# Fetches in tasks of their own, an output norm in place and convolution taps from the bank, in a two-layer encoder trunk

## The chip, the cores and the metric

One core of one Trainium2 chip runs the whole program as one launch. The metric is device time in microseconds, median of the runs. The engines named below are TensorE (matmuls and transposes, PE in the rows; PEld is its weight load), VectorE (DVE), ScalarE (ACT), GpSimd (POOL) and SyncE (SP), which issues every DMA of this kernel. Each engine works through its own list of instructions in order.

## The reference, cut to what matters

Two layers over 2048 frames of width 1024, float32. Each layer normalises its input, projects it once, runs two groups of four heads on the projection, and adds an output projection to its input.

```python
def hybrid_layer(x, ...):
    proj = rmsnorm(x, norm_w) @ w_in          # split: mq mk mv mi mf mz | aq ak av az
    qk = silu(causal_conv(concat(mq, mk), conv_w, conv_b))     # 4 taps, depthwise
    hm = mlstm_chunkwise(mq_c, mk_c, mv, mi + i_bias, mf + f_bias)
    ym = (rmsnorm(hm, m_norm_w) + m_skip * mq_c) * silu(mz)
    ha = diff_attention(rope(aq), rope(ak), av, lam)           # softmax1 - lam*softmax2, causal by chunks of 64
    ya = rmsnorm(ha, a_norm_w) * (1 - lambda_init) * silu(az)
    return x + concat(ym, ya) @ w_out
```

A final norm closes the trunk.

## The kernel before

Rows are worked in stages of 512 frames: 2 layers x 4 stages. A stage has 4 units, one per head u of both groups, so there are 32 units. A unit has projections (convolution of q and of k, the two gates, the values and the rotated q and k of the next unit), scores and softmax maps of the attention head, its product with V, and the mLSTM recurrence over four blocks of 128. After unit 3 of a stage the first half of the output projection (`outproj`, units 0 and 1) runs, merged with `prep_t`, which brings the next stage's 512 x 1024 rows in, scales them by their row norm (line 258), transposes them on TensorE and splits them into a high part (line 264) and a low part (line 266). The second half of the output projection runs in unit 1 of the next stage.

Every float32 matmul is made of three matmuls of split operands. Weights come by DMA into `wr` and are split by ScalarE (line 184) and GpSimd (line 186).

The PSUM banks with the tag `mm` are three; all projections, the output projection and the transposes of `prep_t` take turns in them. Tags in `BUFS` say how many buffers a tile name has: `x` (rows of the next stage) 4, `bc` (row factors of the recurrence) 1, `gza` (the attention gate) 1, `yta` (the normed attention output) 1, `tmp` 4, `yha` and `yla` (the split output of a unit) 2.

Around the change:
- `prep_t`, lines 255 to 259: at the first and the fifth of its eight tasks four half-rows of 128 x 512 are issued and multiplied, and the transposes of four tasks read them.
- `proj_conv`, lines 382 to 396: ScalarE copies the finished bank into `raw` behind three halo columns, which frees the bank; VectorE makes a first pass (line 390) and three taps (line 393) from `raw`; `silu2` follows, whose first step is line 374 on ScalarE.
- `mlstm.begin`, lines 535 to 551: the row factors, 512 KB, are read back from DRAM with a broadcast (line 537), and VectorE (line 539) and ScalarE (line 543) use them at once. For unit 0 they are written in the gates of the same stage (line 515).
- `finish`, lines 762 to 793: `factors` multiplies the attention output with the gate into `yta` (line 778); `spread`, planned 5.5 later, multiplies it with the row norms and splits it (lines 612 and 614). The next unit's gate is written at line 375.

The order comes from a plan. The loop at the end of `trunk_kernel` puts each task at a planned time, tasks are emitted in the order of these times, and matmuls of one stream keep that order. Inside these bounds a scheduler orders each engine's instructions by priority and by readiness in its own model of durations.

Of the kernel before, what the change touches and what calls it, by code (L numbers as in the profile page):

```python
# [38 lines left out]
VD = 3.0  # L39
VL = 0.6  # L40
FD = 5.5
MD = 9.0
MS = 4.2
HA = 150

# [5 lines left out]
def trunk_kernel(ctx, tc, x, w_ch, w_v0, w_v, w_o, nw, cw, cb, gb, mnw, msk, anw, lam,  # L51
# [7 lines left out]
    dr = ctx.enter_context(tc.tile_pool(name="dr", bufs=1, space=bass.MemoryType.DRAM))  # L59

    BUFS = dict(x=4, hth=8, htl=8, wr=3, wh=3, wl=3, yhm=3, ylm=3, yha=2, yla=2, kc=1, vc=2,
                kp=3, vp=3, q=2, raw=1, p=15, ath=2, atl=2, ab=2, tmp=4, xr=2, bc=1, ot=1, ytm=1, yta=1,
                mq=1, mk=1, gzm=1, gza=1, vaug=2, st=1, kw=1, hs=1, hsn=1, aj=1)
    PB = dict(mm=3, sc=2, tpa=1, pv=1, ml=1)

# [40 lines left out]
    def tr(o, i, n=P):  # L106
        pin(PE.transpose(o, i, ident[:n, :n]))  # L107
# [132 lines left out]
    def prep_t(l, t, rs, H, rows=None):  # L240
        pr = par[l]
        src = xin(l, t)
        xs = []

        def task(dc):
            def f():
                if dc == 0:
                    H["rope"] = sb.tile([P, 2, T], F32, tag="rope", name="rope", bufs=1)
                    SY.dma_start(H["rope"], rope[t])
                half, j = divmod(dc, 4)  # L250
                if rows:
                    xs[:] = [r_[half] for r_ in rows]
                elif j == 0:
                    xs.clear()
                    for tb in range(4):
                        xt = st([P, T], "x")
                        SY.dma_start(xt, src[tb * P:(tb + 1) * P, half * T:(half + 1) * T])
                        V.tensor_scalar(out=xt, in0=xt, scalar1=rs()[tb], scalar2=None, op0=ALU.mult)
                        xs.append(xt)
                ps = pst("mm", [P, T])  # L260
                for tb in range(4):
                    tr(ps[:, tb * P:(tb + 1) * P], xs[tb][:, j * P:(j + 1) * P])
                h = st([P, T], "hth", F32R)
                A.activation(h, ps, AF.Copy, scale=pr["nw"][:, dc:dc + 1])
                lo = st([P, T], "htl", F32R)
                V.scalar_tensor_tensor(out=lo, in0=ps, scalar=pr["nw"][:, dc:dc + 1], in1=f32(h),
                                       op0=ALU.mult, op1=ALU.subtract)
                H["hh"].append(h)
                H["hl"].append(lo)
            return f  # L270

        return [(0.44, task(dc)) for dc in range(8)]


# [102 lines left out]
    def proj_conv(l, u, qk, H, X):  # L377

        pr = par[l]

        def post(ps):
            halo = pr["halo"][u]
            raw = st([P, T + 3], "raw")
            A.activation(raw[:, 3:], ps, AF.Copy)
            A.activation(raw[:, 0:3], halo[:, qk], AF.Copy)
            A.activation(halo[:, qk], raw[:, T:], AF.Copy)
            ch = qk * NH + u
            w = lambda j: pr["cw"][:, ch * 4 + j:ch * 4 + j + 1]
            acc = st([P, T], "tmp", name="cacc")
            V.tensor_scalar(out=acc, in0=raw[:, 3:], scalar1=w(3), scalar2=pr["cb"][:, ch:ch + 1],  # L390
                            op0=ALU.mult, op1=ALU.add)
            for j in (2, 1, 0):
                V.scalar_tensor_tensor(out=acc, in0=raw[:, j:j + T], scalar=w(j), in1=acc, op0=ALU.mult, op1=ALU.add)  # L393
            nm = "mq" if qk == 0 else "mk"
            X[nm] = st([P, T], nm)
            silu2(X[nm], acc)

        return proj_ch(l, u, qk, H, post)
# [132 lines left out]
    def mlstm(l, u, X, Y):  # L531
        pr = par[l]
        c = {}

        def begin():
            bc = st([P, 2, 4, P], "bc")
            SY.dma_start(bc.rearrange("p a b i -> p a (b i)"), Y["bwd"][:, u * T:(u + 1) * T].partition_broadcast(P))
            c["dec"] = sm(4, "dec")
            V.tensor_copy(c["dec"], bc[:, 1, :, P - 1])
            wt = c["wt"] = bc[:, 0]  # L540
            cols = Y["cols"]
            for tb in range(4):
                A.activation(wt[:, tb], wt[:, tb], AF.Exp, bias=cols[:, 4 * u + tb:4 * u + tb + 1])
            G.affine_select(out=wt, in_=wt, pattern=[[0, 4], [1, P]], compare_op=ALU.is_ge, fill=0.0,
                            base=0, channel_multiplier=-1)
            c["qw"] = bc[:, 1].rearrange("p b i -> p (b i)")
            G.tensor_tensor(c["qw"], c["qw"], X["mq"], op=ALU.mult)
            c["sk"] = st([P, T], "ytm")
            A.activation(c["sk"], X["mq"], AF.Copy, scale=pr["msk"][:, u:u + 1])
            c["hs"] = st([P, 4, P + 1], "hs")  # L550
            c["ss"] = sm(4, "mss")
# [53 lines left out]
        ts_ = []  # L605
        for tb in range(4):
            ts_ += [lambda tb=tb: s1(tb), lambda tb=tb: s2(tb)]
        return begin, ts_, norm, out_

    def split_y(y, kind):  # L610
        yh = st([P, T], "yh" + kind, F32R)
# [145 lines left out]
    def finish(l, t, u, X):  # L757

        pr = par[l]
        c = {}  # L760

        def factors():

            ot, zz = X["ot"], X["zz"]
            ss = sm(4, "ass")
            ps = pst("tpa", [P, 4, P])
            for qb in range(4):
                tr(ps[:, qb], ot[:, qb * P:(qb + 1) * P])
            for qb in range(4):
                junk = st([P, P], "aj", BF16)  # L770
                A.activation(junk, ps[:, qb], AF.Square, accum_out=ss[:, qb:qb + 1])  # L771
            r = c["r"] = sm(4, "ar")
            V.tensor_tensor(r, zz[:, :, 0], zz[:, :, 0], op=ALU.mult)
            V.tensor_scalar(out=ss, in0=ss, scalar1=1.0 / P, scalar2=None, op0=ALU.mult)
            V.scalar_tensor_tensor(out=r, in0=r, scalar=EPS, in1=ss, op0=ALU.mult, op1=ALU.add)
            G.tensor_tensor(r, r, mhalf, op=ALU.pow)
            y = c["y"] = st([P, T], "yta")
            V.scalar_tensor_tensor(out=y, in0=ot, scalar=pr["anw"][:, 0:1], in1=X["gza"], op0=ALU.mult, op1=ALU.mult)
            if (l, t, u) == units[-1]:

                X["r"] = r
                X["ya"] = split_y(y, "a")

        def spread():

            if (l, t, u) == units[-1]:
                return
            y = c["y"]
            ps = pst("tpa", [P, 4, P])
            for qb in range(4):  # L790
                tr(ps[:, qb], c["r"][:, qb:qb + 1].to_broadcast([P, P]))
            V.tensor_tensor(y, y, ps.rearrange("p a b -> p (a b)"), op=ALU.mult)
            X["ya"] = split_y(y, "a")

        return factors, spread


# [161 lines left out]
    for k in range(-1, N + 1):  # L959
# [6 lines left out]
        if k >= 1:  # L966
# [7 lines left out]
            at(fin_t[k - 1], spread, "V")  # L974
            att += 1.1 * len(v1) + 0.88
        segs = []
        tm = None
        if cur:
            l, t, u = cur
            s = l * n_t + t  # L980
            H, X = Hs[s], Xs[k]
            q0, q1 = scores(l, t, u, X, 0), scores(l, t, u, X, 1)
            v0 = apply_v(l, t, u, X, 0)
            att += total(q0) + total(q1) + 1.1 * len(v0)
            if u == 2 and s < last:
                at(xc, lambda s=s: rs0.__setitem__(s + 1, prep_x((s + 1) // n_t, (s + 1) % n_t)))
            segs.append((0.0, proj_conv(l, u, 0, H, X) + proj_conv(l, u, 1, H, X)))
            if u == 1 and s > 0:
                pl, pt_ = divmod(s - 1, n_t)
                segs.append((fin_t[k - 2] + 6.0, outproj(pl, pt_, 1, Xs[k - 3:k - 1])))  # L990
                if pl == n_layers - 1:
                    segs.append((0.0, [(0.0, lambda pl=pl, pt_=pt_: final(pl, pt_))]))
            segs.append((0.0, proj_gate(l, u, 2, H, X, "gzm")))
            segs.append((0.0, proj_gate(l, u, 3, H, X, "gza")))
            if u == NH - 1 and s < last:
                op = outproj(l, t, 0, Xs[k - 3:k - 1])
                segs.append((fin_t[k - 2] + 6.0, op[:len(op) // 4]))

                pt = prep_t((s + 1) // n_t, (s + 1) % n_t, lambda s=s: rs0[s + 1], Hs[s + 1])
                segs.append((0.0, merge(pt, op[len(op) // 4:])))  # L1000
        elif k == -1:
            segs.append((0.0, prep_first(Hs[0])))
        if nxt:
# [17 lines left out]
        rate = (pe + att) / pe if pe else 1.0  # L1021
        for i, (nb, g) in enumerate(segs):
            xc = max(xc, nb)
            xc = put(g, xc, xc + total(g) * rate)
            if i == 0:
                tm = xc
# [3 lines left out]
        if cur:  # L1030
# [10 lines left out]
            if u == 0:  # L1041
                a = max(t0 + 0.5, me_)
                for g in gates(l, t, X, Ys[s]):
                    at(a, g)
                    a += 3.5
                a = max(a, tm + MD)
            begin, ms, norm, out_ = mlstm(l, u, X, Ys[s])
            at(a, begin)
            a += 4.5
            for f in ms:  # L1050
# [99 lines left out]
```

## Time and profile before

| what | value |
|---|---|
| median of 3 runs | 2933.03 us (2927.04 to 2936.75) |
| the profiled execution's own time | 2937.63 us |
| its span, first to last instruction | 2935.9 us |
| TensorE busy | 2711.7 us, 92% |
| VectorE busy | 1952.4 us, 66% |
| ScalarE busy | 1643.6 us, 56% |
| GpSimd busy | 1467.7 us, 50% |
| mean granted TensorE clock | 0.968 of full speed |

Times in the rows are microseconds from the start of the span, durations of one instruction in a group are nanoseconds. An engine that is idle before an instruction waits for another engine or a DMA, which the rows name behind an arrow.

### The profile page before, as it was taken

The page shows a single profiled execution, that of the slowest core. Times are in us where ns is not written, and L with a number is a line of the kernel's source. Part 1 is how long each engine was busy: PE and PEld are TensorE (multiplying, and loading weights), DVE is VectorE, ACT ScalarE, POOL GpSimd, SP SyncE. Part 2 cuts the span into 40 slices and gives each one's busy share as a digit, 9 for nine tenths or more (in the row PEclk, how much of TensorE's full clock was granted, in tenths as well). Part 3 has the DMA queues.
Part 4 walks back from the last instruction along what each step waited for, and adds up shares of the span by engine and source line. Part 5 has one row for each costly group of instructions (what it writes and reads, how often), then busy time and mean ns, then how long its engine had stood idle before and what let it go on. Part 6 is the DMA issues. An engine that isn't in the chain of part 4 may idle for free. (4 is left out here: it accounts for less than half of the span.)

```text
span 2935.9 us, 48969 instructions
## 1 busy us (share of the span) xinstructions
PE 2711.7 (92%) x16692; PEld 2395.2 (82%) x16692; DVE 1952.4 (66%) x4695; ACT 1643.6 (56%) x4471; POOL 1467.7 (50%) x1182
## 2 busy tenths in 40 slices
PE   7999899999999899999999999999989998998997
PEld 5788788887887888888888887888878887887877
DVE  5566576676757767567855566766677677776684
ACT  4555465555655556555555454555455555665564
POOL 5565656544454344434455655555543545435324
PEclk9999999999999999999999999999999999999998
DMA  6545654463544444434446454654546444364232
GB/s 197 156 130 162 183 157 149 142 200 109 173 140 126 155 116 140 117 99 133 145 130 184 135 175 137 196 167 144 166 127 218 137 140 140 110 186 143 83 107 87
DMA packets 241755, 428.91 MB, mean 146 GB/s; under 512 B 30304, under 2 KB 92768, under 8 KB 241504
## 3 DMA queue, kind: packets, MB, share of 16 engines
q1 hardware_dynamic: 241504, 425.77, 48.5%
q8 instruction: 132, 2.16, 0.3%
q14 instruction: 119, 0.97, 0.1%
HBM read 312.28 MB, written 63.05 MB: 128 GB/s over the span
## 5 line engine op out<-in xcount | busy, mean ns | idle before, releaser
L186 POOL TENSOR_TENSOR wl<-wr,wh 128x512 fp32r<-128x512 f32 (+1 forms) x676 | 919.1, 1366 | 1113.2 <-ACT wh L184 508.5
L104 PE MATMUL mm<-hth,wh 128*128 128x512 f32 x1536 | 629.8, 410 | 1.9 <-ACT vaug L327 1.4
L184 ACT ACTIVATE wh<-wr 128x512 fp32r<-128x512 f32 (+1 forms) x676 | 421.2, 627 | 354.8 <-PE mm L104 219.4
L104 PE MATMUL mm<-htl,wh 128*128 128x512 f32 x1536 | 617.6, 402 | 0.0
L692 DVE TENSOR_SCALAR_CACHE_REDUCE p<-sc 128x512 f32<-128x512 f32 (+3 forms) x640 | 382.0, 605 | 135.0 <-PE sc L104 113.3
L655 ACT ACTIVATE p<-p,nm 128x512 f32<-128x512 f32 (+3 forms) x640 | 413.5, 649 | 102.2 <-DVE nm L651 101.8
L104 PE MATMUL mm<-hth,wl 128*128 128x512 f32 x1536 | 449.8, 407 | 0.0
L104 PEld LDWEIGHTS mm<-hth,wh 128*128 128x128 f32 x1536 | 296.3, 193 | 61.6 <-ACT vaug L327 1.6
L104 PEld LDWEIGHTS mm<-hth,wl 128*128 128x128 f32 x1536 | 291.7, 195 | 62.5 <-POOL wl L186 0.2
L104 PEld LDWEIGHTS mm<-htl,wh 128*128 128x128 f32 x1536 | 295.9, 193 | 57.1
L669 DVE SCALAR_TENSOR_TENSOR p<-p,s 128x512 f32<-128x512 f32 (+2 forms) x320 | 303.0, 992 | 2.1
L104 PE MATMUL mm<-wh,hth 128*128 128x256 f32 (+1 forms) x1024 | 269.0, 292 | 18.4 <-DVE gt L329 10.9
L741 ACT ACTIVATE ath<-tpa 128x512 fp32r<-128x512 f32 x288 | 170.1, 590 | 185.3 <-PE tpa L107 184.4
L742 DVE TENSOR_TENSOR atl<-tpa,ath 128x512 fp32r<-128x512 f32 x288 | 196.9, 684 | 111.9 <-ACT ath L741 110.4
L104 PE MATMUL mm<-wh,htl 128*128 128x256 f32 (+1 forms) x1024 | 264.8, 288 | 0.0
L104 PE MATMUL sc<-kp,q 128*128 128x512 f32 x768 | 247.3, 409 | 7.0 <-DVE p L692 6.8
L393 DVE SCALAR_TENSOR_TENSOR cacc<-raw,cw,cacc 128x512 f32<-128x512 f32 x192 | 218.8, 1140 | 4.4
L104 PEld LDWEIGHTS mm<-wh,hth 128*128 128x128 f32 x1024 | 199.4, 195 | 24.5 <-issue 9.4
L104 PEld LDWEIGHTS mm<-wh,htl 128*128 128x128 f32 x1024 | 199.5, 195 | 2.6
L107 PE MATMUL tpa<-ident,p 128*128 128x128 f32 x1088 | 189.7, 281 | 9.2 <-DVE tpa L734 7.6
L104 PE MATMUL pv<-ath,vp 128*128 128x256 f32 x768 | 181.7, 290 | 7.3 <-ACT ath L741 7.2
L104 PE MATMUL mm<-wl,hth 128*128 128x256 f32 (+1 forms) x1024 | 164.2, 289 | 0.0
(203 smaller groups left out, 5684.2 us busy)
## 6 DMA issues: line engine op xcount, KB each, us to landing
wr<-in_w_ch_dram SPq DMA_DIRECT2D x384, 256.0 KB, 2.8
wr<-in_w_o_dram SPq DMA_DIRECT2D x132, 256.0 KB, 2.9
q<-ab SPq DMA_DIRECT2D x256, 128.0 KB, 2.4
vp<-vd SPq DMA_DIRECT2D x48, 512.0 KB, 4.0
wr<-in_w_v_dram SPq DMA_DIRECT2D x96, 256.0 KB, 3.0
kp<-kd SPq DMA_DIRECT2D x48, 512.0 KB, 4.2
wr<-in_w_v_dram SPq DMA_DIRECT2D x64, 264.0 KB, 3.4
kc<-ab SPq DMA_DIRECT2D x256, 64.0 KB, 2.0
```

The source lines that it names most:

```text
L104: pin(PE.matmul(o, l, r, start=start, stop=stop, skip_group_check=True))
L107: pin(PE.transpose(o, i, ident[:n, :n]))
L184: A.activation(wh[:, :n], wr[:, :n], AF.Copy)
L186: G.tensor_tensor(wl[:, :n], wr[:, :n], f32(wh[:, :n]), op=ALU.subtract)
L393: V.scalar_tensor_tensor(out=acc, in0=raw[:, j:j + T], scalar=w(j), in1=acc, op0=ALU.mult, op1=ALU.add)
L655: A.activation(pp[:, :w], pp[:, :w], AF.Exp, bias=nm[:, m:m + 1], accum_out=zc[:, m, kt:kt + 1])
L669: V.scalar_tensor_tensor(out=pc[0][kt][:, :w], in0=pc[1][kt][:, :w], scalar=s_[:, 0:1], in1=pc[0][kt][:, :w], op0=ALU.mult, op1=ALU.add)
L692: V.tensor_scalar(out=pp[:, :w], in0=ps[:, :w], scalar1=0.125, scalar2=None, op0=ALU.mult, op1=ALU.max, accum_out=c["mx"][:, m, kt:kt + 1])
L741: A.activation(ah, p2, AF.Copy)
L742: V.tensor_tensor(al, p2, f32(ah), op=ALU.subtract)
```

## The change

Four edits go together.

- `prep_t` issues rows by quarters of 256 columns, two blocks of 128 rows in a tile; the first two quarters have a task of their own, 10 (XD) ahead of the planned start of the merged segment, and the other two are issued as soon as the first two have been transposed. The multiplies are 256 wide.
- The row factors are fetched by a task of their own, 9 (BD) ahead of `begin`, into one of two buffers. For unit 0 `begin` is planned 9 later than before.
- `proj_conv` no longer has `raw`: ScalarE makes the first tap from the bank (scale and bias), VectorE adds three taps that read the bank, each with a small one for the columns that need the halo, and the halo is copied from the bank at the end.
- `finish` writes the normed output into the gate's own buffer, so `yta` goes.

```diff
-                kp=3, vp=3, q=2, raw=1, p=15, ath=2, atl=2, ab=2, tmp=4, xr=2, bc=1, ot=1, ytm=1, yta=1,
+                kp=3, vp=3, q=2, p=15, ath=2, atl=2, ab=2, tmp=4, xr=2, bc=2, ot=1, ytm=1,
...
+        def fetch(q):
+
+            qs[q] = [st([P, 2, 256], "x") for _ in range(2)]
+            for i, xt in enumerate(qs[q]):
+                SY.dma_start(xt, src[2 * i * P:2 * (i + 1) * P, q * 256:(q + 1) * 256].rearrange("(b p) c -> p b c", p=P))
...
-                    for tb in range(4):
-                        xt = st([P, T], "x")
-                        SY.dma_start(xt, src[tb * P:(tb + 1) * P, half * T:(half + 1) * T])
-                        V.tensor_scalar(out=xt, in0=xt, scalar1=rs()[tb], scalar2=None, op0=ALU.mult)
-                        xs.append(xt)
+                    if j == 0:
+                        for tb in range(4):
+                            xb = qs[q][tb // 2][:, tb % 2]
+                            V.tensor_scalar(out=xb, in0=xb, scalar1=rs()[tb], scalar2=None, op0=ALU.mult)
+                    xs = [qs[q][tb // 2][:, tb % 2, j * P:(j + 1) * P] for tb in range(4)]
...
+                if not rows and j == 1 and q < 2:
+                    fetch(q + 2)
             return f
...
+        H["fetch"] = lambda: (fetch(0), fetch(1))
...
-            raw = st([P, T + 3], "raw")
-            A.activation(raw[:, 3:], ps, AF.Copy)
-            A.activation(raw[:, 0:3], halo[:, qk], AF.Copy)
-            A.activation(halo[:, qk], raw[:, T:], AF.Copy)
...
-            V.tensor_scalar(out=acc, in0=raw[:, 3:], scalar1=w(3), scalar2=pr["cb"][:, ch:ch + 1],
-                            op0=ALU.mult, op1=ALU.add)
+            A.activation(acc, ps, AF.Identity, scale=w(3), bias=pr["cb"][:, ch:ch + 1])
             for j in (2, 1, 0):
-                V.scalar_tensor_tensor(out=acc, in0=raw[:, j:j + T], scalar=w(j), in1=acc, op0=ALU.mult, op1=ALU.add)
+
+                d = 3 - j
+                V.scalar_tensor_tensor(out=acc[:, d:], in0=ps[:, 0:T - d], scalar=w(j), in1=acc[:, d:],
+                                       op0=ALU.mult, op1=ALU.add)
+                V.scalar_tensor_tensor(out=acc[:, 0:d], in0=halo[:, qk, j:3], scalar=w(j), in1=acc[:, 0:d],
+                                       op0=ALU.mult, op1=ALU.add)
+            A.activation(halo[:, qk], ps[:, T - 3:T], AF.Copy)
...
+        def fetch():
+            bc = c["bc"] = st([P, 2, 4, P], "bc")
+            SY.dma_start(bc.rearrange("p a b i -> p a (b i)"), Y["bwd"][:, u * T:(u + 1) * T].partition_broadcast(P))
...
-            y = c["y"] = st([P, T], "yta")
+            y = c["y"] = X["gza"]
...
+            if i in fetches:
+                at(xc - XD, fetches[i]["fetch"])
...
-                a = max(a, tm + MD)
-            begin, ms, norm, out_ = mlstm(l, u, X, Ys[s])
+                a = max(a + BD, tm + MD)
+            fetch, begin, ms, norm, out_ = mlstm(l, u, X, Ys[s])
+            at(a - BD, fetch)
             at(a, begin)
```

## Rows read from the trace of the kernel before

**Rows 1.** The page: busy time of each engine, share of the span.

```profile
PE 2711.7 (92%) x16692; PEld 2395.2 (82%) x16692; DVE 1952.4 (66%) x4695; ACT 1643.6 (56%) x4471; POOL 1467.7 (50%) x1182
```

**Rows 2.** Waits of TensorE: total us, times, longest us.

```profile
PE pv L104 <- DVE atl L742: 61.8, 37, 5.5
PE sc L104 <- DVE p L692: 24.1, 14, 3.6
PE mm L107 <- DVE x L258: 17.1, 12, 3.8
```

**Rows 3.** Waits of ScalarE, VectorE and SyncE, from their three tables.

```profile
ACT th L374 <- DVE cacc L393: 98.0, 39, 4.5
ACT bc L543 <- DMA bc<-bw: 82.1, 30, 6.1
...
DVE dec L539 <- DMA bc<-bw: 62.1, 23, 6.8
...
SPq L537 <- PE ml L104: 33.8, 18, 3.7
```

**Rows 4.** Timeline of unit 28: start us, duration us, what, idle before.

```profile
2508.66 0.38 SPq L537 DMA_DIRECT2D bc<-bw  x1
...
2517.59 0.17 DVE L539 COPY dec<-bc 128x4 f32<-128x4 f32 x1 [5.36 <-DMA bc<-bw]
...
2518.36 0.71 PE L104 MATMUL sc<-kp,q 128*128 128x512 f32 x1 [3.48 <-DVE p L692]
```

**Rows 5.** Windows after gaps (PEclk third from the end): one, then three sums.

```profile
197.40:200.70 3.30, 3.30 (x15) 3.20 (x16) 2.04 (x5) 3.27 (x9) 0.74 (x1) 0.50 0.92 333
...
sum 33.30, PE 30.64 PEld 25.70 DVE 22.53 ACT 18.04 POOL 15.94; mean PE 3.83 PEld 3.21 DVE 2.82 ACT 2.26 POOL 1.99
...
sum 9.90, PE 9.90 PEld 8.48 DVE 6.52 ACT 9.62 POOL 7.22; mean PE 3.30 PEld 2.83 DVE 2.17 ACT 3.21 POOL 2.41
...
sum 23.50, PE 22.36 PEld 20.28 DVE 21.11 ACT 7.38 POOL 0.66; mean PE 3.73 PEld 3.38 DVE 3.52 ACT 1.23 POOL 0.11
```

**Rows 6.** Windows: a gate waiting for its buffer; seven stage ends, their sum.

```profile
954.00:975.00 21.00, 21.00 (x168) 20.35 (x168) 15.15 (x48) 12.85 (x35) 3.83 (x3) 1.00 0.40 130
...
sum 260.40, PE 234.76 PEld 223.06 DVE 194.90 ACT 155.17 POOL 89.95; mean PE 33.54 PEld 31.87 DVE 27.84 ACT 22.17 POOL 12.85
```

**Rows 7.** Timeline of TensorE: first and last gap of one kind.

```profile
197.35 0.47 PE L107 MATMUL ml<-ident,hs 128*128 128x128 f32 x1 [2.00 <-ACT hs L593]
...
2765.92 0.38 PE L104 MATMUL pv<-ath,vp 128*128 128x256 f32 x1 [1.39 <-ACT ath L741]
```

**Rows 8.** Lines 257 and 258 by source: ns min/median/max, first and last start.

```profile
L257 SPq DMA_DIRECT2D x<-in_x_dram x24: 327/355/1932, 29.3 to 984.9; - x24
...
DMA to landing us min/median/max: 2.7/4.6/7.0
...
L258 DVE TENSOR_SCALAR x<-x,rs x32: 470/486/1565, 1008.0 to 2438.9; 128x512 f32<-128x512 f32 x32
```

**Rows 9.** VectorE lines 393, 266 and 583 by source: ns min/median/max.

```profile
L393 DVE SCALAR_TENSOR_TENSOR cacc<-raw,cw,cacc x192: 664/753/1837, 62.2 to 2815.8; 128x512 f32<-128x512 f32 x192
...
L266 DVE SCALAR_TENSOR_TENSOR htl<-mm,nw,hth x64: 731/743/753, 18.2 to 2456.6; 128x512 fp32r<-128x512 f32 x64
...
L583 DVE SCALAR_TENSOR_TENSOR den<-hs x32: 143/159/1157, 128.2 to 2851.5; 128x4 f32<-128x4 f32 x32
```

**Rows 10.** Groups by line: busy us, mean ns | idle before.

```profile
L393 DVE SCALAR_TENSOR_TENSOR cacc<-raw,cw,cacc 128x512 f32<-128x512 f32 x192 | 218.8, 1140 | 4.4
...
L390 DVE TENSOR_SCALAR cacc<-raw,cw,cb 128x512 f32<-128x512 f32 x64 | 62.1, 971 | 74.0 <-ACT raw L384 56.3 <-POOL wl L186 13.2 <-POOL bc L547 2.8
```

**Rows 11.** Timeline: the gate and the split of one stage end.

```profile
1402.91 0.67 DVE L375 SCALAR_TENSOR_TENSOR gza<-th,mm 128x512 f32<-128x512 f32 x1
...
1430.18 1.28 POOL L614 TENSOR_TENSOR yla<-yta,yha 128x512 fp32r<-128x512 f32 x1
```

More of the change, by code (lines that the diff above doesn't have):

```diff
@@ L41 @@
 FD = 5.5
+XD = 10.0
 MD = 9.0
+BD = 9.0
 MS = 4.2
@@ L242, in prep_t @@
         src = xin(l, t)
-        xs = []
+        qs = {}
+        def fetch(q):
+            qs[q] = [st([P, 2, 256], "x") for _ in range(2)]
+            for i, xt in enumerate(qs[q]):
+                SY.dma_start(xt, src[2 * i * P:2 * (i + 1) * P, q * 256:(q + 1) * 256].rearrange("(b p) c -> p b c", p=P))
         def task(dc):
@@ L249, in f @@
                     SY.dma_start(H["rope"], rope[t])
-                half, j = divmod(dc, 4)
+                q, j = divmod(dc, 2)
                 if rows:
-                    xs[:] = [r_[half] for r_ in rows]
-                elif j == 0:
-                    xs.clear()
-                    for tb in range(4):
-                        xt = st([P, T], "x")
-                        SY.dma_start(xt, src[tb * P:(tb + 1) * P, half * T:(half + 1) * T])
-                        V.tensor_scalar(out=xt, in0=xt, scalar1=rs()[tb], scalar2=None, op0=ALU.mult)
-                        xs.append(xt)
+                    xs = [r_[dc // 4][:, (dc % 4) * P:(dc % 4 + 1) * P] for r_ in rows]
+                else:
+                    if j == 0:
[3 more added lines that the diff above has]
+                    xs = [qs[q][tb // 2][:, tb % 2, j * P:(j + 1) * P] for tb in range(4)]
                 ps = pst("mm", [P, T])
                 for tb in range(4):
-                    tr(ps[:, tb * P:(tb + 1) * P], xs[tb][:, j * P:(j + 1) * P])
+                    tr(ps[:, tb * P:(tb + 1) * P], xs[tb])
                 h = st([P, T], "hth", F32R)
@@ L533, in mlstm @@
         c = {}
+        def fetch():
+            bc = c["bc"] = st([P, 2, 4, P], "bc")
+            SY.dma_start(bc.rearrange("p a b i -> p a (b i)"), Y["bwd"][:, u * T:(u + 1) * T].partition_broadcast(P))
         def begin():
-            bc = st([P, 2, 4, P], "bc")
-            SY.dma_start(bc.rearrange("p a b i -> p a (b i)"), Y["bwd"][:, u * T:(u + 1) * T].partition_broadcast(P))
+            bc = c["bc"]
             c["dec"] = sm(4, "dec")
@@ L607, in mlstm @@
             ts_ += [lambda tb=tb: s1(tb), lambda tb=tb: s2(tb)]
-        return begin, ts_, norm, out_
+        return fetch, begin, ts_, norm, out_
     def split_y(y, kind):
@@ L976, in trunk_kernel @@
         segs = []
+        fetches = {}
         tm = None
@@ L1000, in trunk_kernel @@
                 segs.append((0.0, merge(pt, op[len(op) // 4:])))
+                fetches[len(segs) - 1] = Hs[s + 1]
         elif k == -1:
```

## Prediction

> **What bounds the kernel.** I read the page's engine table first: TensorE is busy 2711.7 of 2935.9 us, 92%, and the next engine, VectorE, 66% [rows 1]. The reader should see that TensorE sets the pace and that at most the remaining 224 us of its idle time, and whatever its clock loses, can be had; no other engine's saving counts unless it shortens a TensorE wait. So the second view is the table of waits for TensorE: no single cause stands out; the largest are evictions of VectorE (61.8 us for the attention product, 24.1 us for scores) and the scaled rows of the next stage (17.1 us) [rows 2]. The third is the same table for the engines that TensorE waits for: ScalarE and VectorE stand idle 82.1 and 62.1 us for the DMA of the row factors, and ScalarE another 98.0 us for the convolution's taps [rows 3]. Both engines take their instructions in order, so an eviction queued behind such a wait is late too. The timeline of one case shows it whole: VectorE is idle for 5.36 us at the factors' first reader, then a score group on TensorE that had waited 3.48 us for a VectorE eviction queued behind it [rows 4]. [...]
>
> **Row factors (fetch apart from use, two buffers).** I followed TensorE's gaps over 0.9 us back through the queue of the engine that ended each. Behind fifteen of them stands the factors' DMA: nine in units 1 to 3 of a stage, 18.6 us together (first 2.00 us, last 1.39 us), and six in unit 0, 13.5 us (the last of 3.48 us) [rows 4, 7]. Slow stretches follow eight of the first kind, 33.3 us long, so 16.7 us lost, and three of the second, 9.9 us, so 5.0 us [rows 5]. Together 35.3 us for units 1 to 3 and 18.5 us for unit 0.
> What the fetch needs differs. In units 1 to 3 the factors have long been in DRAM; what held the DMA was the one buffer (SyncE waited 33.8 us, 18 times, for the recurrence's matmul that reads it last [rows 3]). With two buffers and a task of its own, nothing holds it: a DMA whose buffer is free does go out early here, since the first rows of stage 1 were issued at 29.3 us for a use some 250 us later [rows 8]. In unit 0 the gates of the same stage have only just written the factors (line 515), so the fetch cannot move up; instead the first use is planned 9 units of plan time later, against a landing of 8.9 us in this case (issue 2508.66, reader 2517.59) [rows 4]. But the order on an engine is by readiness in the planner's model, and an engine that the model sees idle will still be given the waiting instruction. So I count unit 0 at a third, 6.2 us, units 1 to 3 at 0.6, 21.2 us. The 0.6 is a choice between ends: 1.0 if TensorE keeps every microsecond, 0.2 if it runs into the next late eviction, of which 61.8 us are there [rows 2].
>
> **Next stage's rows by quarters.** The old code loads four half-rows, uses them in four tasks, and only then finds free buffers for the second half. The first half is issued far ahead, so only the second half stalls: TensorE's 12 waits for line 258, 17.1 us [rows 2], with six slow stretches of 23.5 us after them, so 11.8 us [rows 5]. Landing takes 4.6 us in the median [rows 8]. After the change a quarter's buffers are free after two tasks, and the refill is needed two tasks later; a stage end of some 37 us, the mean of seven [rows 6], has eight such tasks merged with the output projection, so two tasks are some 9 us by this, enough for a landing of 4.6 us (7.0 us at most) and four multiplies of 0.3 to 0.6 us. The multiplies double in number (56 to 112, 256 wide instead of 512): between half of 486 ns each and the same [rows 8], 0 to 27 us more on VectorE, 4 us in one stage end at worst, where VectorE is busy 194.90 of 260.40 us [rows 6]. I count 0.6 of 28.9 us, 17.3 us.
>
> **Convolution from the bank.** Removed: one 512-wide pass of VectorE at 971 ns and one tiny ScalarE copy per convolution (64 of them); the ScalarE copy of the bank becomes the first tap, the same pass over the same bank, so no change. The three remaining taps read the bank instead of a copy, and each gets a head of 1 to 3 columns. The old taps took 664 to 1837 ns with a mean of 1140, 218.8 us in all plus 62.1 us for the first pass [rows 9, 10]. A VectorE operation of the same kind with one operand in PSUM, the low part of the rows (line 266), keeps between 731 and 753 ns. Two-operand operations of 4 columns in SBUF, the nearest to a head, took 143 to 1157 ns, median 159 [rows 9]. So after: 192 x 745 ns, 143 us, plus 192 heads, 31 us at the median and 222 us at the worst; before 281 us. I take heads at twice the median, 61 us: about 77 us less of VectorE, 4% of its busy time. On TensorE this is worth 4% of the 85.9 us that it waits for evictions of VectorE [rows 2], 3.4 us, and part of ScalarE's 98.0 us for the taps, 2.5 us in each of 39 waits, of which a shorter chain takes 1 us each; I count 8 us in all, between a loss of 5 (heads at their worst) and a gain of 25.
> [...]
> The bank is held about 3 us longer. Cover: there are three banks, and TensorE did 168 matmuls in 21 us [rows 6], so a group of 24 takes 3 us and two groups, 6 us, pass before the bank is needed; with this cover gone, 0.5 us at each of 64 would be 32 us.
>
> **Output norm in place.** Removed: one buffer, no instruction. What it adds is a wait. The gate buffer is now read until the split at line 614, and the next unit's gate may be written (line 375) only then; the projection's bank, one of three, waits with it. In the case shown the gate was written at 1402.91 and the split ended at 1431.46 [rows 11]: it would be held 28.6 us longer. In seven stage ends this is 260.4 us, the stretches summed in [rows 6]. Queued behind line 375 on VectorE are evictions, and behind the bank the output projection and the transposes. That hurts only if two banks do not do. They did: from 954 to 975 us a gate already waited for its buffer, the projection's fills ran on two banks, and TensorE was busy 21.00 of 21.00 us at clock 1.00 [rows 6]. I count a loss of 5 us, between 0 and 60.
>
> **Sum.** 21.2 + 6.2 + 17.3 + 8 - 5 = 48 us off the profiled execution's own 2937.6 us, 2890 us. That execution lies 4.6 us above the median of the runs shown, so I forecast 2885 us.
>
> **Rivals.** (1) The gate's bank decides, and it gets slower: each of 14 fills in seven stage ends waits. For one VectorE pass of an eviction, 743 ns (line 266 [rows 9]), that is 98 waits and 73 us in place of my 5 us: 2953 us. It turns from gain to loss at 0.5 us a fill. For it: TensorE is idle 25.6 of the 260.4 us there already [rows 6]. Against: the 21 us without a gap [rows 6]. 0.17.
> (2) The waits move on: with factors and rows there in time, TensorE meets the next late eviction and keeps 0.2 of the 83 us, 17 us, and nothing of the taps: 2933 - 17 + 5, 2921 us. For it: 61.8 us of evictions spread over 37 waits [rows 2]. Against: the slow clock after a gap goes away with it. 0.17.
> [...] 0.08.
> (4) Everything is kept: 35.3 + 18.5 + 28.9 + 25 us off the median, 2825 us. 0.08.
> My forecast, 2855 to 2912 us by itself, has 0.50.
>
> **Range and chances.** About 0.3%, 9 us, is what a measurement here can tell from no change. Below 2924: the forecast, (3), (4) and half of (2), 0.75; within: the other half of (2) and a little of (1), 0.10; slower: 0.15. From 2840 (between (4) and the forecast) to 2945 (into (1)) some 2 in 10 are left out.
>
> **What would show it.** Right: waits for the factors' DMA fall from 82.1 and 62.1 us to under 35 each, what is left in unit 0; no TensorE wait for scaled rows but a few us; taps at 660 to 760 ns with no tail; fewer stretches at 0.50; TensorE's idle time by the page down from 224 to about 195 us. Wrong: a new TensorE wait for a bank at the stage ends or VectorE idle before line 375 for the split's POOL pass beyond 40 us (rival 1); idle for evictions growing by what the factors gave (rival 2); heads near 1 us each. The forecast fails most likely if the planner's new order of work on ScalarE and VectorE makes waits that no row here shows.

## The result, and the profile after

The changed kernel takes 2855.45 us (median, 2853.26 to 2860.85), against 2930.03 us of the kernel before on the same chips: a ratio of 0.9746, 95% interval 0.9721 to 0.9772. It is 75 us faster; 48 us were forecast.

The page of the changed kernel, its span and the engines' busy time, answers to [rows 1]. Its line numbers are up to 19 higher than before: 104 is now 106, 537 is 548, 539 is 553, 543 is 557, 258 is 265, 266 is 273, 375 is 385, 614 is 628.

```profile
span 2853.7 us, 49241 instructions
...
PE 2675.9 (94%) x16692; PEld 2376.0 (83%) x16692; DVE 1873.5 (66%) x4879; ACT 1641.3 (58%) x4407; POOL 1422.6 (50%) x1182
```

TensorE has the same 16692 matmuls, and its idle time (span less busy) fell from 224.2 to 177.8 us, by 46.4. Its busy time fell too, by 35.8 us: the same matmuls at a higher mean clock, 0.980 after 0.968. The two together are the 82.2 us by which the span of the profiled execution is shorter. By the clock records of the two traces TensorE stood at 0.50 in 43 stretches before, 188.8 us together, and in 25 after, 115.1 us; at 1.00 otherwise. Half of the 73.7 us between them is 36.9 us, near the 35.8. So almost half of the gain came as clock.

The waits of TensorE (total us, times, longest), the answer to [rows 2]:

```profile
PE pv L106 <- DVE atl L756: 52.8, 35, 5.6
...
PE mm L106 <- DVE htl L273: 14.8, 7, 4.0
PE sc L106 <- DVE p L706: 11.7, 14, 2.5
PE mm L106 <- DVE xr L855: 8.6, 9, 1.9
...
PE mm L109 <- DVE xr L855: 3.1, 2, 1.8
```

The 24.1 us for scores have halved, and the 17.1 us for scaled rows have gone from the list. New are the waits for VectorE's split of the rows (htl) and for its sum behind the output projection (xr). In all 20 of them, at the seven stage ends, the matmul or transpose that waits reads neither tile; it waits for the PSUM bank that VectorE is still reading. With 2.1 us more for htl at line 109 they are 28.6 us, against 1.8 us before (0.2 us of them at line 107):

```profile
PE mm L104 <- DVE htl L266: 0.9, 2, 0.5
...
PE mm L104 <- DVE xr L841: 0.7, 1, 0.7
```

The waits of ScalarE, VectorE and SyncE, the answer to [rows 3]:

```profile
ACT halo L404 <- DVE cacc L402: 81.5, 46, 3.3
...
ACT bc L557 <- DMA bc<-bw: 58.5, 26, 4.4
...
DVE x L265 <- DMA x<-in_x_dram: 20.1, 11, 4.2
...
DVE dec L553 <- DMA bc<-bw: 18.3, 7, 4.6
...
DVE x L265 <- DMA x<-xo: 10.1, 9, 2.2
DVE gza L385 <- POOL yla L628: 9.5, 9, 1.8
...
SPq L548 <- PE ml L106: 17.1, 11, 3.7
```

The reader is to see five things: VectorE's wait for the factors fell from 62.1 to 18.3 us, ScalarE's only from 82.1 to 58.5; VectorE now waits 30.2 us for the next stage's rows (20.1 and 10.1) where it waited 25.2 before (13.7 and 11.5); the gate's new wait for the split is 9.5 us; ScalarE's wait for the taps, 98.0 us before, is 81.5 us and now stands before the halo's copy (line 404); and SyncE still waits 17.1 us, where it waited 33.8, for a factor buffer to come free.

### The profile page after: what moved, and what is told of

The parts are those of the page before. It is cut to its first block, busy times and chain, and to the rows that moved or that the text cites. A ratio compares the mean times of both kernels' runs of the same rounds, so it can differ in the third digit from the quotient of the medians.

```text
span 2853.7 us, 49241 instructions
## 1 busy us (share of the span) xinstructions
PE 2675.9 (94%) x16692; PEld 2376.0 (83%) x16692; DVE 1873.5 (66%) x4879; ACT 1641.3 (58%) x4407; POOL 1422.6 (50%) x1182
## 5 line engine op out<-in xcount | busy, mean ns | idle before, releaser
L188 POOL TENSOR_TENSOR wl<-wr,wh 128x512 fp32r<-128x512 f32 (+1 forms) x676 | 898.9, 1335 | 1131.2 <-PE mm L106 523.3
L106 PE MATMUL mm<-hth,wh 128*128 128x512 f32 x1536 | 621.7, 405 | 1.6 <-ACT vaug L337 1.4
L106 PE MATMUL mm<-htl,wh 128*128 128x512 f32 x1536 | 610.4, 397 | 0.0
L106 PE MATMUL mm<-hth,wl 128*128 128x512 f32 x1536 | 442.5, 401 | 0.0
L106 PEld LDWEIGHTS mm<-hth,wl 128*128 128x128 f32 x1536 | 285.4, 190 | 60.9
L683 DVE SCALAR_TENSOR_TENSOR p<-p,s 128x512 f32<-128x512 f32 (+2 forms) x320 | 293.3, 962 | 2.3
L400 DVE SCALAR_TENSOR_TENSOR cacc<-mm,cw,cacc 128x511 f32<-128x511 f32 (+2 forms) x192 | 141.5, 737 | 72.2 <-ACT cacc L396 68.9
```

Of the source, the lines that this page charges most:

```text
L106: pin(PE.matmul(o, l, r, start=start, stop=stop, skip_group_check=True))
L188: G.tensor_tensor(wl[:, :n], wr[:, :n], f32(wh[:, :n]), op=ALU.subtract)
L400: V.scalar_tensor_tensor(out=acc[:, d:], in0=ps[:, 0:T - d], scalar=w(j), in1=acc[:, d:], op0=ALU.mult, op1=ALU.add)
L683: V.scalar_tensor_tensor(out=pc[0][kt][:, :w], in0=pc[1][kt][:, :w], scalar=s_[:, 0:1], in1=pc[0][kt][:, :w], op0=ALU.mult, op1=ALU.add)
```

## The experiments

Each is a kernel beside the one before on the same chip. Ratios are to that kernel, with 95% intervals.

**One part alone.** Three kernels are the one before with one edit of the diff each (rows by quarters; convolution from the bank; norm in place). The fourth is the changed kernel with the factors' part taken back:

```diff
-tmp=4, xr=2, bc=2,
+tmp=4, xr=2, bc=1,
...
+            bc = st([P, 2, 4, P], "bc")       # fetched in begin again
...
-                a = max(a + BD, tm + MD)
+                a = max(a, tm + MD)
```

> The kernel before with the rows by quarters alone. Fetch theory (the two fetches give most of the 75 us): 15 to 25 us faster, TensorE's 17.1 us of waits for the scaled rows gone and half of their slow stretches. VectorE theory (the convolution's relief gives most, and VectorE still waits 30 us for these DMAs, only elsewhere): within 8 us of before.

Measured: 2935.72 us, ratio 1.0007 (0.9994 to 1.0020). Nothing, as the second theory had it. VectorE waited 15.8 and 16.1 us for the rows' DMA, not less than before. TensorE's wait for scaled rows went, but its idle time stayed (224.5 us after 224.2): it waited longer for evictions of the attention and the recurrence (atl 68.0 us after 61.8, ath 22.6 after 15.8, hs 17.7 after 9.8).

> The kernel before with the convolution from the bank alone. Fetch theory: 5 to 12 us faster. VectorE theory: 30 to 45 us faster, with VectorE's busy time down by 40 to 80 us. If the bank held longer hurts: slower, with a TensorE wait for a bank behind the taps.

Measured: 2898.28 us, 0.9875 (0.9855 to 0.9896), 36 us faster, with VectorE's busy time at 1880.7 us, 72 us down. No TensorE wait for a bank appeared behind the taps.

> The kernel before with the output norm in place alone. Both theories: 0 to 8 us slower, from VectorE's wait before the gate for the split on GpSimd and from two banks at the stage ends. Rival 1 of the prediction: 40 us slower or more.

Measured: 2909.97 us, 0.9920 (0.9902 to 0.9939). It is 23 us faster; neither theory had that. TensorE's idle time fell by 24.5 us and its busy time by 4.4, so here the clock gave little (0.972 after 0.968). Its waits for a bank (htl and xr, as above) rose from 1.8 to 7.2 us.

> The changed kernel with the factors' part undone (one buffer, DMA in begin, unit 0 at its old plan). Fetch theory: 25 to 40 us slower than the changed kernel, so 35 to 50 us faster than before. VectorE theory: 5 to 15 us slower than the changed kernel, so 60 to 70 us faster than before, as ScalarE's wait for the factors is only 82.1 against 58.5 us.

Measured: 2907.71 us, 0.9916 (0.9893 to 0.9939). So the factors' part is worth about 50 us in the changed kernel, more than either theory gave it, and the other three parts together are worth 25, less than the convolution alone.

**A control, and two edits taken apart.** Parts that do not add up ask how much a new order of instructions alone moves the time. Two kernels change one constant of the plan, `MD = 9.0` to `MD = 9.4`, before and after. One gives the changed kernel a single buffer again (`bc=1`, fetch task and plan as changed), and one gives the norm in place two gate buffers (`gza=2`).

> A control: the kernel before with one constant of the plan (MD, the recurrence's delay after the convolution) at 9.4 in place of 9.0 and nothing else. Wait theory (each edit is worth the waits that it takes away, so a nudge without a wait is worth nothing): within 9 us of before. Order theory (a new order on ScalarE and VectorE alone moves the time by as much as the single edits did): 10 to 30 us off, to either side.

Measured: 2942.43 us, 1.0031 (1.0011 to 1.0050), 9 us slower. VectorE's busy time moved by 20 us all the same (1932.2 after 1952.4).

> The same control on the changed kernel. Wait theory: within 9 us of the changed kernel's 2855 us. Order theory: 10 to 30 us off, and rather slower, as the changed kernel may be a fortunate order.

Measured: 2843.09 us, 0.9678 (0.9654 to 0.9703), against 0.9746 of the changed kernel: faster, where slower was expected. A plan constant that was not meant to take any wait away moved the time by 9 us to one side and, by the ratios, 20 us to the other (12 us by the medians). These are two nudges only. From here on a difference under 20 us between two kernels is not put down to its edit.

> The changed kernel with one buffer for the factors; the fetch task and the plan of unit 0 stay. If the second buffer is what the factors' part gives (the fetch of units 1 to 3 goes out 40 to 80 us before its use in the changed kernel): back to the 2895 to 2916 us of the kernel without the factors' part. If the task ahead in the plan gives it: within 12 us of the changed kernel.

Measured: 2909.08 us, 0.9908 (0.9884 to 0.9932): all of the part's gain is gone. The task ahead and unit 0's later plan, which this kernel keeps, give nothing (0.9916 without them). By the profiled executions the second buffer is worth 30.9 us of TensorE's idle time and 27.1 us of its busy time (208.7 and 2703.0 us with one). The waits of ScalarE and VectorE in it:

```profile
ACT bc L557 <- DMA bc<-bw: 87.1, 29, 5.6
DVE dec L553 <- DMA bc<-bw: 68.1, 31, 5.3
```

Where the second buffer pays is seen in unit 13 (layer 0, stage 3, head 1), one unit in which much was gained, from the start of its first projection to that of the next unit's. The window of the one-buffer kernel, and then that of the changed one (length; busy us and number for TensorE, its weight loads, VectorE, ScalarE, GpSimd; granted clock; DMA):

```profile
1115.20:1244.90 129.70, 117.10 (x724) 104.14 (x723) 80.71 (x198) 72.20 (x200) 52.27 (x42) 0.93 0.46 134
```

```profile
1096.50:1210.40 113.90, 109.86 (x727) 99.15 (x726) 77.24 (x195) 73.05 (x204) 52.73 (x43) 1.00 0.50 153
```

Nearly the same work takes 15.8 us less: 8.6 us less idle and 7.2 us less busy, at a clock of 1.00 in place of 0.93. In this window the one-buffer kernel waits for the factors of unit 14: they are issued (at 1194.55) only after the last matmul of unit 13 that reads the one buffer, and VectorE stands before them, with a score eviction of TensorE behind it:

```profile
1200.29 0.17 DVE L553 COPY dec<-bc 128x4 f32<-128x4 f32 x1 [2.71 <-DMA bc<-bw]
...
1202.05 0.80 PE L106 MATMUL sc<-kp,q 128*128 128x512 f32 x1 [2.83 <-DVE p L706]
```

In the changed kernel the same factors go out 85 us before VectorE reads them, and VectorE does not wait; ScalarE, which reads them 5 us after the issue, does:

```profile
1087.81 0.38 SPq L548 DMA_DIRECT2D bc<-bw  x1
...
1093.02 1.28 ACT L557 ACTIVATE bc<-bc,cols 128x128 f32<-128x128 f32 x4 [0.99 <-DMA bc<-bw]
...
1173.03 0.26 DVE L553 COPY dec<-bc 128x4 f32<-128x4 f32 x1
```

> The kernel before with the output norm in place and two gate buffers, so that the gate never waits for the split, nor for the multiply that it waited for before. The norm in place alone gave 23 us. If the later gate gave them (TensorE's projections held back, attention first): back to 2933 us within 9 us. If it is the gate's wait that costs, as the prediction has it: faster than 2910 us. Order theory: anywhere between 2900 and 2950 us.

Measured: 2909.79 us, 0.9917 (0.9896 to 0.9938), the same as with one gate buffer. So neither the gate's wait nor a later gate makes the 23 us. TensorE's waits for a bank (htl and xr) are 0.7 us here, against 7.2 us with one gate buffer.

**What is left of the change.** The last four: the changed kernel with the old `prep_t`; two that fix an order between instructions of one engine; and the convolution and the norm in place on the kernel before.

```diff
-                A.activation(wt[:, tb], wt[:, tb], AF.Exp, bias=...)
+                after(A.activation(wt[:, tb], wt[:, tb], AF.Exp, bias=...), X["thmq"])
```

```diff
-                            V.tensor_scalar(out=xb, in0=xb, scalar1=rs()[tb], ...)
+                            m = V.tensor_scalar(out=xb, in0=xb, scalar1=rs()[tb], ...)
+                            if q >= 2:
+                                after(m, H["lo"][2 * q - 2])
```

> The changed kernel with the rows by halves as before. If the quarters give their 17 us here, beside free engines, though they gave none alone: 2867 to 2885 us. If the wait only moved from TensorE to VectorE (30.2 us before the multiplies in the changed kernel, 25.2 before): within 12 us of 2855 us, which is what a nudge of the plan does.

Measured: 2866.10 us, 0.9758 (0.9740 to 0.9776), against 0.9746 with the quarters. They give nothing here either. VectorE waits in it 22.8 us for the rows and TensorE 9.3 us for their scaling, a wait that is gone with the quarters; but its waits for a bank are 8.3 us in place of 28.6, and its idle time is 175.0 us, against 177.8 with the quarters.

> The changed kernel with one order fixed: ScalarE's four exponentials of the factors come after the tanh of the unit's own q, so ScalarE no longer stands before their DMA (58.5 us, 26 times). If a ScalarE wait counts like VectorE's, whose fall from 68 to 18 us went with 54 us: 25 us faster or more, under 2830 us. If TensorE waits for VectorE above all: within 12 us of 2855 us.

Measured: 2850.82 us, 0.9700 (0.9683 to 0.9717). ScalarE's wait for the factors fell from 58.5 to 19.6 us, and 18.4 us came back as its wait for the taps (99.9 after 81.5); the time moved by 13 us at most, within a nudge.

> The changed kernel with one order fixed: VectorE's multiplies of the third and fourth quarter come after the low part of the first task of the quarter before, so the DMA has landed when VectorE reaches them (30.2 us of waits now, about half of them there). If VectorE's waits count one for one: 10 to 20 us faster. If the stage end has other late work behind it: within 8 us, with new TensorE waits for the transposes' rows.

Measured: 2846.49 us, 0.9689 (0.9675 to 0.9703). VectorE's waits for the rows fell from 30.2 to 14.2 us, and the ratio by 0.0057, 17 us: what the first theory expected, but within a nudge too. The trace does not bear that theory out: TensorE's idle time is 178.5 us after 177.8, and its waits for a bank are 27.2 us after 28.6.

> The kernel before with the convolution from the bank and the norm in place, 36 and 23 us alone. If the gate's 23 us are a wait of its own taken away: 50 to 60 us faster than before. If they come from VectorE's idle that the convolution's relief also removes: 25 to 40 us faster. As the kernel with the quarters too was 25 us faster, the second is likelier.

Measured: 2912.32 us, 0.9913 (0.9899 to 0.9928), 25 us faster than before, the lower end of what the second theory expected, and not faster than either edit alone. TensorE's waits for a bank are 14.5 us with both, 2.8 us with the convolution alone and 7.2 us with the norm alone, which may be a part of why the two do not add up.

Put in a row, the ratios are: before 1; convolution and norm 0.9913; with quarters 0.9916; with the fetch task and plan 0.9908; with the second buffer 0.9746. Five kernels with two factor buffers lie between 0.9678 and 0.9758, three with one buffer and both other edits between 0.9908 and 0.9916. The gap between the groups is larger than either nudge. The factors' part alone on the kernel before was not run, so whether it gives as much there is open.

## Why the prediction was right, and where it was not

**What bounds the kernel** held. TensorE's gaps and its slow stretches are where the time came from, 46.4 and 35.8 us, in about the proportion that the prediction gave them (for the gaps behind the factors 32.1 us of idle to 21.7 of clock). The half that the terms take of each slow stretch is the 0.50 of [rows 5], and over the two traces it gives 36.9 us for the 35.8 measured. The share of the clock is no fixed rate: with the norm in place alone it was 24.5 to 4.4.

**Row factors.** The mechanism held, the size did not: this term was put at 27.4 us (21.2 and 6.2) and measured 47 (0.9908 to 0.9746). The choice that failed was the 0.6 kept of 35.3 us: the gaps followed one by one were only those over 0.9 us that stood right behind the DMA, and in the case shown the second buffer gave more than those gaps. In unit 13 of the one-buffer kernel only two gaps of TensorE, 2.83 and 0.61 us, stand right behind the factors' DMA (VectorE waits 2.71 us for it just before the first, ScalarE 3.62 before the second; both are for unit 14's factors): 3.4 of the 8.6 us of idle that went. Two more gaps of about 3 us, for the eviction of attention weights (atl), have no such DMA just behind them and went too: no gap left in the changed kernel's window is over 1.58 us. The work of VectorE and ScalarE was in another order by then; one cause for this remainder was not found. It was right that the one buffer held the DMA in units 1 to 3: VectorE's waits there, some 31 of the 62.1 us, are gone. Unit 0 kept a wait, as forecast: the 18.3 us left on VectorE are seven waits in the eight first units, where some 31 us stood before. It was wrong that nothing would hold the fetch any more (SyncE's wait for a buffer only halved, to 17.1 us), and wrong that ScalarE's wait would fall under 35 us. Its exponentials need only the factors and run as soon as these land: in unit 14 some 80 us before VectorE's copy (1093.02 and 1173.03 in the timeline above), and with a wait in 26 places over the kernel. VectorE's copy did not move forward so far. What is left of ScalarE's wait costs little: taking 39 us of it away moved the time by no more than a nudge, though 18 us came back as ScalarE's wait for the taps. That VectorE's wait was the one that counted fits this, but both fell together with the second buffer, so it is argued, not shown.

**Next stage's rows.** This step failed: 17.3 us forecast, 0 measured alone and under 4 in the changed kernel. The wait of TensorE named in [rows 2] did go, and its idle time did not fall with it. Alone, the wait came back at other evictions. In the changed kernel the multiplies stand on VectorE just behind the DMA and wait there for 30.2 us; what is queued behind them is late, the split of the rows too, which frees a bank: TensorE's waits for a bank are 28.6 us with the quarters and 8.3 without. The prediction counted when the buffers come free and not where the multiplies would stand. That their place is the reason is argued: with their order fixed, VectorE's waits fell by 16.0 us and TensorE's waits for a bank by 1.4.

**Convolution.** VectorE's busy time was forecast 77 us lower; it fell by 78.9 us in the changed kernel and 72 with this edit alone. By source (ns min/median/max), the first tap, the taps and the heads of the changed kernel:

```profile
L396 ACT ACTIVATE cacc<-mm,cb,cw x64: 754/762/781, 58.6 to 2731.2; 128x512 f32<-128x512 f32 x64
...
L400 DVE SCALAR_TENSOR_TENSOR cacc<-mm,cw,cacc x192: 661/737/752, 59.5 to 2734.9; 128x511 f32<-128x511 f32 x64, 128x510 f32<-128x510 f32 x64, 128x509 f32<-128x509 f32 x64
...
L402 DVE SCALAR_TENSOR_TENSOR cacc<-halo,cw,cacc x192: 141/445/1347, 60.2 to 2735.5; 128x1 f32<-128x1 f32 x64, 128x2 f32<-128x2 f32 x64, 128x3 f32<-128x3 f32 x64
```

The taps are what the prediction said, without a tail; heads were put at 318 ns and take 530 in the mean (35.4 + 37.3 + 29.0 us over 192). Taps and heads together come to 243 us, 38 less than before; the rest of VectorE's relief lies in other groups (line 669, the softmax combination, took 308.1 us at its four widths before and 298.5 after), so that 78.9 met 77 is luck, and a nudge alone moved VectorE's busy time by 20 us. The relief of the taps themselves goes with GpSimd's work. Laid against GpSimd's instructions in the timeline of the kernel before, the 74 old taps that met none took 664 to 753 ns, 742 in the mean, and the 68 that ran wholly beside one took 1551 in the mean; taps from the bank, in the changed kernel, take 730 and 738. The prediction had the tail and not what it goes with, and so not that the heads, with both operands in SBUF, would have it too. The shortest tap takes 661 ns from the bank and 664 from SBUF. The first tap was forecast to cost what the copy did, 583 ns in the mean, and takes 767. The copy has no operand that is a column of scales or biases and the first tap has two; line 264 of the kernel before has one and takes 682. No run takes the three apart further. On the whole time the term was mis-sized: 8 us forecast, 36 alone. Beside the norm in place it adds nothing (0.9913 against 0.9920), so its size depends on what else is there.

**Norm in place.** VectorE's wait before line 385 is small, as forecast, 9.5 us. But the bank behind it is held: at the seven stage ends the gate was written 44.6 to 64.7 us after ScalarE's tanh had read its bank, against 0.6 to 26.5 us before. At the first one TensorE waits inside this time for a bank:

```profile
251.55 0.58 ACT L384 ACTIVATE th<-mm 128x512 f32<-128x512 f32 x1
...
271.03 0.58 PE L106 MATMUL mm<-wh,yhm 128*128 128x256 f32 x1 [2.54 <-DVE htl L273]
...
301.18 0.68 DVE L385 SCALAR_TENSOR_TENSOR gza<-th,mm 128x512 f32<-128x512 f32 x1
```

So the prediction's first sign of being wrong, a new TensorE wait for a bank at the stage ends, did appear. Over the whole of each trace these waits are 7.2 to 28.6 us in the nine kernels with the norm in place and one gate buffer, and 0.7 to 5.5 us in the five others, the one with two gate buffers among them. The cover that failed is the two banks: they did in the one stretch of 21 us on which it was read, and not over the seven stage ends. The term of 5 us stands against 26.8 us more of such waits, but rival 1 did not decide, since the kernel got faster. The changed kernel with two gate buffers was not run, so what these waits cost in time is not shown. The sign of the whole term was wrong alone (23 us faster) and is not settled with the convolution there (0.9913 against 0.9875). Why it gains alone stays open: two gate buffers gave the same, so the wait on the gate is not the cause, and what the two kernels share is that the output no longer goes through a buffer of its own. The kernel before with two such buffers was not run. The 23 us are also little more than a nudge.

**Rival 2**, the waits moving on, did not decide, though it is what happened to the rows. The sum fell short by 27 us, 20 of them in the factors' term. That the other three together were forecast at 20 us and measured 25 is luck: alone they gave 0, 36 and 23 us in place of 17, 8 and -5, and they do not add up.

## What to carry to other kernels

Where a scheduler orders by modelled readiness, a fetch that is made earlier can pull its first readers forward too: look at where the readers will stand, and fix their order if the engine that they stand on feeds the bottleneck. A second buffer for data that are read late by one engine and early by another frees the late one, and can be worth more than the idle time that one follows back to it: here almost half of its gain, 27.1 of 58.0 us by the profiled executions, was TensorE's clock. A buffer that is held longer can hold a bank with it: count the banks that are left over all the places where they are filled, and not in one stretch. Before a gain of one edit is believed, nudge a constant that should do nothing: here that moved the time by up to 20 us, and the gains of single edits did not add up.

## What was not expected of the hardware

VectorE operations on one to three columns, with both operands in SBUF, took 141 to 1347 ns, 530 in the mean; a full tap from the bank took 737 in the mean and never longer than 752. The timelines of the changed kernel show when: the 67 that ran while GpSimd had no instruction in flight took 204 ns in the mean and 216 at most, the 90 that ran wholly beside GpSimd's instructions 715 in the mean. GpSimd's spans are rough, so the two groups are too.

The clock's share of the gain was nearly as large as that of the idle time, and in one unit as well as over the whole: 7.2 us beside 8.6 in unit 13, where the granted clock went from 0.93 to 1.00, and 35.8 beside 46.4 in the span.
